# Column means of an 8192 x 8192 matrix: loads in pairs of row groups on two queues, without early loads, the last four groups summed by TensorE alone

## The chip, the cores and the metric

The kernel runs on one core of one Trainium2 chip. The metric is the device time of one execution in microseconds (us). "SyncE", "ScalarE", "GpSimd", "VectorE" and "TensorE" are the engines that the profile writes as SP, ACT, POOL, DVE and PE. "DMA" is the core's 16 DMA engines, which move data between device memory and the on-chip buffers; a transfer is put to them by an instruction on SyncE's or ScalarE's instruction stream.

## The reference

```python
def setup_inputs():
    return {"x": np.random.randn(8192, 8192).astype(np.float32)}

def reference(x):
    return np.mean(x, axis=0)
```

The input is 268.4 MB of float32, every byte of which has to be read once; the output is 32 KB.

## The kernel before

The 8192 rows are 64 groups of 128 rows (`G = 64`, `P = 128`). A group is 4 MB: 128 partitions with a row of 8192 columns each. The buffer `bufs` has six slots of one group each: slots 0 to 3 take loads, slot 4 is `both`, slot 5 is the running sum `acc`. Columns are counted in blocks of `F = 512`; `W = 128`.

**The stream.** A load of two groups (8 MB) lets partition p take two neighbouring rows, so it reads 64 KB in one piece per partition. Two pairs of slots, 0-1 and 2-3, are filled in turn. For each pair VectorE does two adds of 8192 columns: `both = slot + slot`, after which the pair of slots is free, and `acc = acc + both`. Line 96 has all adds of VectorE, line 76 all loads. All loads are issued by SyncE, so they stand in one queue (q1 in the profile). The load into a pair of slots is issued when the `both` add that reads it has ended; the load of the other pair is then still in flight.

**Waits.** An add that needs both a load and the add before it waits for a no-op on another engine (line 99), which waits for the two; the no-ops are on ScalarE and on GpSimd. `declare_no_dep` takes away dependences that such a wait covers already. A load with an even number from 8 on also waits for the loads eight and seven before it (`over`), which have long landed by then.

**The beginning.** The first load brings four groups, the second two more into the slots of `both` and `acc`. Around them SyncE issues two early loads into a tile `early`: columns 14F to 16F of group 60 and 9F to 14F of group 63. GpSimd adds them to `acc` in two pieces in the middle of the stream (line 129).

**The end.** From group 56 on the loads bring one group each. VectorE adds groups 56 to 59, 14 blocks of group 60 and blocks 7 to 15 of group 61. GpSimd adds three blocks of group 62 (line 148). TensorE sums `acc` and what is left of groups 61, 62 and 63 over the partitions (line 183): the matrix `ones`, holding 1/8192, times a block gives sums, in PSUM tiles `bank` (two), `wide`, `two` and `last`. ScalarE copies them out (line 198), VectorE the last one (line 214). Stores are issued by SyncE and ScalarE (line 201; those of ScalarE are q10). Group 63 is loaded in four pieces of 1 MB, 1 MB, 512 KB and 256 KB, so that little work follows the last piece. `keep_in_program_order` keeps the order on an engine as written.

Of the kernel before, what the change touches and what calls it, by code (L numbers as in the profile page):

```python
# [9 lines left out]
def kernel(  # L10
# [2 lines left out]
    x: bass.AP,  # L13
    out: bass.AP,
):

    nc = tc.nc
    f32 = mybir.dt.float32
    M, N = x.shape  # L40
    P = nc.NUM_PARTITIONS
    F = 512
    W = F // 4
    G = M // P
    U = 6
    sync = mybir.DependencyInfo(mybir.DependencyClass.Sync, mybir.DependencyReason.DATA)

    sb = ctx.enter_context(tc.tile_pool(name="sb", bufs=1))
    psp = ctx.enter_context(tc.tile_pool(name="psum", bufs=1, space=bass.MemoryType.PSUM))

    bufs = sb.tile([P, U, N], f32, name="bufs")
    both = bufs[:, U - 2, :]
    acc = bufs[:, U - 1, :]
    ones = sb.tile([P, 32], f32, name="ones")
    early = sb.tile([P, 7 * F], f32, name="early")
    tail = sb.tile([P, W], f32, name="tail")
    warm = sb.tile([P, 32], f32, name="warm")
    nc.gpsimd.memset(ones[:], 1.0 / M)  # L58
    ready = sb.tile([P, 1], f32, name="ready")
    tc.keep_in_program_order(  # L60
        nc.gpsimd.tensor_add(out=ready[:], in0=ones[:, 0:1], in1=ones[:, 1:2]))  # L61
    banks = [psp.tile([P, F], f32, name=f"bank{b}") for b in range(2)]
    wide = psp.tile([P, 2 * F], f32, name="wide")
    two = psp.tile([P, 2 * W], f32, name="two")
    last = psp.tile([P, W], f32, name="last")

    loads = []

    def landed(*inss):

        nop = tc.keep_in_program_order(nc.sync.nop()).ins
        for o in inss:
            tc.add_manual_dep(nop, o.name, sync, reason="SyncE waits")

    def load(dst, src):
        ins = tc.keep_in_program_order(nc.sync.dma_start(out=dst, in_=src)).ins  # L76
        k = len(loads)
        over = loads[k - 8:k - 6] if k >= 8 and k % 2 == 0 else []
        tc.declare_no_dep(ins, group="loads", keep=over, reason="the reader of the buffer waited")
        for o in over:  # L80
            tc.add_manual_dep(ins, o.name, sync, reason="covers the next load too")
        tc.add_to_no_dep_group("loads", ins)
        loads.append(ins)
        return ins

    def rows(g, n=1):
        return x[g * P:(g + n) * P, :]

    def load_rows(g, u, n):
        return load(bufs[:, u:u + n, :], rows(g, n).rearrange("(p j) c -> p j c", j=n))  # L90

    adds, joins = [], {}

    def add(dst, a, b, dmas):

        ins = nc.vector.tensor_add(out=dst, in0=a, in1=b).ins  # L96
        if dmas and adds:
            waiter = nc.scalar if len(adds) % 8 > 1 else nc.gpsimd
            nop = joins[waiter] = tc.keep_in_program_order(waiter.nop()).ins  # L99
            for o in dmas + adds[-1:]:  # L100
                tc.add_manual_dep(nop, o.name, sync, reason="the no-op waits")
            for group in ("loads", "adds"):
                tc.declare_no_dep(ins, group=group, reason="the no-op waited")
            tc.add_manual_dep(ins, nop.name, sync, reason="waits for both at once")
        elif adds:
            tc.declare_no_dep(ins, group="loads", reason="the add ahead waited")
        tc.declare_no_dep(ins, group="early", reason="the no-op waited, or the add behind it")
        tc.add_to_no_dep_group("adds", ins)
        adds.append(ins)

    load(early[:, 5 * F:], rows(G - 4)[:, 14 * F:])
    first, second = load_rows(0, 0, 4), load_rows(4, 4, 2)
    load(early[:, :5 * F], rows(G - 1)[:, 9 * F:14 * F])
    add(bufs[:, 2:4, :], bufs[:, 2:4, :], bufs[:, 0:2, :], [first])
    add(bufs[:, 4:6, :], bufs[:, 4:6, :], bufs[:, 2:4, :], [second])
    add(acc, acc, both, [])
    tc.keep_in_program_order(nc.scalar.copy(out=warm[:], in_=ones[:]))  # L117
    ahead = []
    g = 6
    while g < G - 8:  # L120
        u = (g + 2) % 4
        dma = load_rows(g, u, 2)
        add(both, bufs[:, u, :], bufs[:, u + 1, :], [dma])
        add(acc, acc, both, ahead)
        ahead = []
        if g in (24, 32):
            lo, hi = (0, 4) if g == 24 else (4, 7)
            cols = slice((9 + lo) * F, (9 + hi) * F)
            ins = tc.keep_in_program_order(nc.gpsimd.tensor_add(  # L129
                out=acc[:, cols], in0=acc[:, cols], in1=early[:, lo * F:hi * F])).ins  # L130
            tc.add_to_no_dep_group("early", ins)
            ahead = [ins]
        g += 2

    while g < G - 4:
        row = bufs[:, (g + 2) % 4, :]
        add(acc, acc, row, [load(row, rows(g))])
        g += 1
    for lo, hi, loaded in [(0, 14, 14), (7, 16, 16)]:
        row = bufs[:, (g + 2) % 4, :]  # L140
        dma = load(row[:, :loaded * F], rows(g)[:, :loaded * F])
        cols = slice(lo * F, hi * F)
        add(acc[:, cols], acc[:, cols], row[:, cols], [dma])
        g += 1
    r61, r62, r63 = [bufs[:, (g + 1 + j) % 4, :] for j in range(3)]
    load(r62, rows(g))
    for cols in [slice(14 * F, 16 * F), slice(8 * F, 9 * F)]:
        joined = tc.keep_in_program_order(nc.gpsimd.tensor_add(  # L148
            out=acc[:, cols], in0=acc[:, cols], in1=r62[:, cols])).ins
    g += 1  # L150
    for lo, hi in [(4, 8), (0, 4), (14, 16), (8, 9)]:
        load(r63[:, lo * F:hi * F], rows(g)[:, lo * F:hi * F])

    sums = []

    def blocks(row, lo, hi):
        for i in range(lo, hi):
            sums.append((banks[i // 4], i % 4, 0, row[:, i * F:(i + 1) * F]))

    def spread(dst, row, lo, hi, part=slice(None)):  # L160
        n = (hi - lo) * W
        for c in range(0, n, F)[part]:
            for q in range(4):
                at = lo * F + q * n + c
                sums.append((dst, q, c, row[:, at:at + min(F, n - c)]))

    blocks(acc, 2, 5)
    blocks(acc, 0, 2)
    blocks(r61, 0, 7)
    blocks(acc, 5, 8)  # L170
    blocks(r62, 0, 8)
    spread(wide, acc, 9, 14, slice(1))
    blocks(r63, 4, 8)
    spread(wide, r62, 9, 14, slice(1))
    for row in (acc, r62):
        spread(wide, row, 9, 14, slice(1, 2))
    spread(two, acc, 14, 16)
    blocks(r63, 0, 4)
    spread(last, acc, 8, 9)
    spread(two, r63, 14, 16)  # L180
    spread(last, r63, 8, 9)
    for n, (dst, q, c, cols) in enumerate(sums):
        summed = tc.keep_in_program_order(nc.tensor.matmul(  # L183
            out=dst[32 * q:32 * q + 32, c:c + cols.shape[1]],
# [5 lines left out]
            skip_group_check=True,  # L190
        )).ins

    res = both[:, :2 * F].rearrange("p (b c) -> p b c", b=2)
    res5 = both[:, 2 * F:2 * F + 5 * W]
    res2 = both[:, 4 * F:4 * F + 2 * W]

    def copy(dst, src):
        return tc.keep_in_program_order(nc.scalar.copy(out=dst, in_=src)).ins  # L198

    def store(engine, dst, src, *then):  # L200
        ins = tc.keep_in_program_order(engine.dma_start(out=dst, in_=src)).ins
        for o in then:
            tc.add_manual_dep(ins, o.name, sync, reason="follows that load")
        return ins

    def part(lo, hi):
        return out[lo * F:hi * F].rearrange("(q c) -> q c", q=4)

    copy(res[:, 1, :], banks[1][:])
    s1 = store(nc.scalar, part(4, 8), res[0:P:32, 1, :], loads[-4])  # L210
    copy(res5, wide[:, :5 * W])
    copy(res[:, 0, :], banks[0][:])
    copied = copy(res2, two[:])
    ended = nc.vector.tensor_copy(out=tail[:], in_=last[:]).ins  # L214
    landed(*joins.values())
    s5 = store(nc.sync, part(9, 14), res5[0:P:32, :], *loads[-7:-3])
    s0 = store(nc.sync, part(0, 4), res[0:P:32, 0, :])
    s2 = store(nc.scalar, part(14, 16), res2[0:P:32, :])
    store(nc.sync, part(8, 9), tail[0:P:32, :])
    landed(loads[-2], joined)  # L220
    landed(loads[-1], copied)
    landed(s0, s5)
    landed(s1, summed)
    landed(s2, ended)
    hold = tc.keep_in_program_order(nc.vector.nop()).ins
    tc.add_manual_dep(hold, s0.name, sync, reason="VectorE ends late")

# [29 lines left out]
```

## Time and profile before

| | |
|---|---|
| time, median of 3 runs | 628.55 us (627.99 to 628.99) |
| profiled execution, span from first to last instruction | 626.4 us |
| what lies around the span (runs less span) | 1.6 to 2.6 us, 2.15 at the median |
| read from device memory | 268.44 MB, 429 GB/s over the span |
| VectorE busy | 529.3 us (85%) |
| TensorE busy | 13.3 us (2%) |
| ScalarE, GpSimd busy | 3.7 us, 12.0 us |
| granted TensorE clock | 1.000 |

The time of the profiled execution is not listed apart from the three runs; its span is the part that the profile explains. The DMA share is the mean busy share of the 16 DMA engines, and can pass 1 in a short window, because a packet counts where it starts. A wait is shown with the instruction that released it. A value such as "DVE bufs<-bufs L96" names the engine, the output and input tiles and the line. The profile records a float32 matmul of this kernel twice, so its 126 records are 63 matmuls of the program.

### The profile page before, as it was taken

The numbers are of one execution on the slowest core, as the hardware profiler recorded it, in microseconds if no ns is written. First come the engines' busy times: TensorE is split into PE (matmuls) and PEld (weight loads), VectorE is DVE, ScalarE is ACT, GpSimd is POOL, SyncE is SP. The second block draws the span as 40 slices with busy tenths as digits, with TensorE's granted clock in tenths as the row PEclk, the third lists the DMA queues.
The fourth block names the chain that finished last, engine by engine and source line by source line (L and its number), as shares of the span: only waits on it lengthen the run. The fifth ranks groups of instructions, "written<-read, shape, count | busy, mean of one in ns | idle before, by whom it ended". The sixth has DMA issues, their size and how long they took to land.

```text
span 626.4 us, 484 instructions
## 1 busy us (share of the span) xinstructions
PE 13.3 (2%) x126; PEld 4.0 (1%) x126; DVE 529.3 (85%) x60; ACT 3.7 (1%) x6; POOL 12.0 (2%) x10
## 2 busy tenths in 40 slices
PE   0000000000000000000000000000000000000008
PEld 0000000000000000000000000000000000000002
DVE  0028999998888998889998899888898888999992
ACT  0000000000000000000000000000000000000001
POOL 0000000000000000020000200000000000000002
PEclk9999999999999999999999999999999999999999
DMA  8999999999999999999999999999999999999997
GB/s 372 465 402 428 459 410 460 402 469 402 469 402 469 402 469 402 469 402 469 402 465 406 439 431 427 444 410 460 402 469 402 469 402 469 402 435 435 419 435 305
DMA packets 5930, 268.50 MB, mean 429 GB/s; under 512 B 660, under 2 KB 668, under 8 KB 1064
## 3 DMA queue, kind: packets, MB, share of 16 engines
q1 hardware_dynamic: 5912, 268.46, 99.3%
q8 instruction: 1, 0.02, 0.0%
q10 hardware_dynamic: 16, 0.01, 0.0%
q14 instruction: 1, 0.01, 0.0%
HBM read 268.44 MB, written 0.03 MB: 429 GB/s over the span
## 4 chain that ended last, share of the span: by engine, by line
DMA 59%; DVE 30%; another core or an unknown queue 10%; issue 0%; SPq 0%; ACTq 0%; PE 0%; POOL 0%; POOLq 0%
DMA bufs<-in_x_dram 59%; DVE bufs L96 30%; SPq L76 0%; ACTq L99 0%; PE last L183 0%; DVE tail L214 0%; POOL ready L61 0%; POOL ones L58 0%; POOLq L99 0%; POOLq L241 0%
## 5 line engine op out<-in xcount | busy, mean ns | idle before, releaser
L96 DVE TENSOR_TENSOR bufs<-bufs 128x8192 f32<-128x8192 f32 (+3 forms) x59 | 529.0, 8966 | 85.9 <-DMA bufs<-in_x_dram 43.0
L183 PE MATMUL bank<-bufs,ones 128*32 128x512 f32 x62 | 10.0, 716 | 610.3 <-DVE bufs L96 610.0
L129 POOL TENSOR_TENSOR bufs<-bufs,early 128x2048 f32<-128x2048 f32 (+1 forms) x2 | 7.9, 3954 | 348.5 <-DVE bufs L96 348.5
L148 POOL TENSOR_TENSOR bufs<-bufs 128x1024 f32<-128x1024 f32 (+1 forms) x2 | 3.6, 1824 | 258.9 <-DMA bufs<-in_x_dram 258.9
L214 DVE COPY tail<-last 128x128 f32<-128x128 f32 x1 | 0.3, 291 | 8.8 <-PE last L183 8.8
L183 PEld LDWEIGHTS bank<-bufs,ones 128*32 128x32 f32 x62 | 2.2, 121 | 616.4 <-issue 614.5
L198 ACT COPY bufs<-bank 128x512 f32<-128x512 f32 x2 | 1.2, 586 | 617.9 <-PE bank L183 617.9
L183 PE MATMUL wide<-bufs,ones 128*32 128x512 f32 (+1 forms) x32 | 2.5, 432 | 0.0
L117 ACT ACT_TABLE_LOAD x1 | 1.3, 1283 | 0.7 <-PEq L241 0.7
L183 PE MATMUL two<-bufs,ones 128*32 128x256 f32 x16 | 1.2, 380 | 0.0
L183 PEld LDWEIGHTS wide<-bufs,ones 128*32 128x32 f32 x32 | 1.0, 110 | 1.8 <-issue 1.8
L183 PE MATMUL last<-bufs,ones 128*32 128x128 f32 x16 | 0.8, 279 | 0.1
L198 ACT COPY bufs<-wide 128x640 f32<-128x640 f32 x1 | 0.7, 692 | 1.1 <-PE wide L183 1.1
L183 PEld LDWEIGHTS last<-bufs,ones 128*32 128x32 f32 x16 | 0.4, 109 | 1.2 <-issue 0.6
L183 PEld LDWEIGHTS two<-bufs,ones 128*32 128x32 f32 x16 | 0.4, 109 | 0.1
L198 ACT COPY bufs<-two 128x256 f32<-128x256 f32 x1 | 0.4, 372 | 0.1
L117 ACT COPY warm<-ones 128x32 f32<-128x32 f32 x1 | 0.2, 217 | 0.0
L61 POOL TENSOR_TENSOR ready<-ones 128x1 f32<-128x1 f32 x1 | 0.2, 193 | 0.1
L58 POOL MEMSET ones<- 128x32 f32 x1 | 0.1, 125 | 0.3 <-POOLq L241 0.3
L241 POOL MEMSET const-float32-0.0<- 128x1 f32 x1 | 0.1, 98 | 0.2 <-issue 0.2
L241 POOL MEMSET const-bfloat16-1.0<- 128x1 bf16 x1 | 0.1, 102 | 0.0
L241 POOL MEMSET const-uint8-127<- 128x1 uint8 x1 | 0.1, 102 | 0.0
(1 smaller groups left out, 0.1 us busy)
## 6 DMA issues: line engine op xcount, KB each, us to landing
bufs<-in_x_dram SPq DMA_DIRECT2D x6, 4096.0 KB, 20.4
bufs<-in_x_dram SPq DMA_DIRECT2D x1, 3584.0 KB
bufs<-in_x_dram SPq DMA_DIRECT2D x2, 1024.0 KB, 18.7
early<-in_x_dram SPq DMA_DIRECT2D x1, 1280.0 KB
early<-in_x_dram SPq DMA_DIRECT2D x1, 512.0 KB
bufs<-in_x_dram SPq DMA_DIRECT2D x1, 512.0 KB, 19.4
bufs<-in_x_dram SPq DMA_DIRECT2D x27, 29.9
bufs<-in_x_dram SPq DMA_DIRECT2D x1, 256.0 KB, 19.7
```

What stands on the lines that cost most here:

```text
L58: nc.gpsimd.memset(ones[:], 1.0 / M)
L61: nc.gpsimd.tensor_add(out=ready[:], in0=ones[:, 0:1], in1=ones[:, 1:2]))
L96: ins = nc.vector.tensor_add(out=dst, in0=a, in1=b).ins
L117: tc.keep_in_program_order(nc.scalar.copy(out=warm[:], in_=ones[:]))
L129: ins = tc.keep_in_program_order(nc.gpsimd.tensor_add(out=acc[:, cols], in0=acc[:, cols], in1=early[:, lo * F:hi * F])).ins
L148: joined = tc.keep_in_program_order(nc.gpsimd.tensor_add(out=acc[:, cols], in0=acc[:, cols], in1=r62[:, cols])).ins
L183: summed = tc.keep_in_program_order(nc.tensor.matmul(out=dst[32 * q:32 * q + 32, c:c + cols.shape[1]], lhsT=ones[:], rhs=cols, start=all(( ...
L198: return tc.keep_in_program_order(nc.scalar.copy(out=dst, in_=src)).ins
L214: ended = nc.vector.tensor_copy(out=tail[:], in_=last[:]).ins
L241: nc = _bacc.Bacc("TRN2", target_bir_lowering=False, num_devices=1)
```

## The change

Loads 0 to 30 bring two groups each; load 31 brings group 62, loads 32 to 35 the pieces of group 63 (2 MB, 1.25 MB, 512 KB, 256 KB). Loads 3, 5, ... 29 are issued by ScalarE, all others by SyncE, so in the stream slots 0-1 are filled from SyncE's queue and slots 2-3 from ScalarE's. Each load still waits for the `both` add that read its slots. The early loads, the first load of four groups, the single-group loads and all adds of GpSimd are gone. All no-ops ahead of adds are on GpSimd. VectorE adds groups 0 to 59 with 59 adds of 8192 columns; TensorE sums groups 60, 61, `acc`, 62 and 63 in that order, 24 matmuls each, 120 in all. VectorE also copies one of the two 512-column results. The results have tiles of their own, and the stores have no added waits on loads.

```diff
     def load(dst, src):
-        ins = tc.keep_in_program_order(nc.sync.dma_start(out=dst, in_=src)).ins
         k = len(loads)
+        engine = nc.scalar if 2 <= k < G // 2 - 1 and k % 2 else nc.sync
+        ins = tc.keep_in_program_order(engine.dma_start(out=dst, in_=src)).ins
         over = loads[k - 8:k - 6] if k >= 8 and k % 2 == 0 else []
...
-            waiter = nc.scalar if len(adds) % 8 > 1 else nc.gpsimd
+            waiter = nc.gpsimd
...
-    load(early[:, 5 * F:], rows(G - 4)[:, 14 * F:])
-    first, second = load_rows(0, 0, 4), load_rows(4, 4, 2)
-    load(early[:, :5 * F], rows(G - 1)[:, 9 * F:14 * F])
...
+    def pair(g):
+        u = g % 4
+        dma = load(bufs[:, u:u + 2, :], rows(g, 2).rearrange("(p j) c -> p j c", j=2))
+        return bufs[:, u, :], bufs[:, u + 1, :], dma
+
+    a, b, dma = pair(0)
+    add(acc, a, b, [dma])
     tc.keep_in_program_order(nc.scalar.copy(out=warm[:], in_=ones[:]))
...
+    for g in range(2, G - 4, 2):
+        a, b, dma = pair(g)
+        add(both, a, b, [dma])
+        add(acc, acc, both, [])
+    r60, r61, _ = pair(G - 4)
+    r62, r63 = bufs[:, 2, :], bufs[:, 3, :]
+    load(r62, rows(G - 2))
+    for lo, hi in [(0, 8), (8, 13), (13, 15), (15, 16)]:
+        load(r63[:, lo * F:hi * F], rows(G - 1)[:, lo * F:hi * F])
...
+    for row in (r60, r61, acc, r62, r63):
+        blocks(banks[0], row, 0)
+        blocks(banks[1], row, 4)
+        spread(banks[2], row, 8, 5)
+        spread(banks[3], row, 13, 2)
+        spread(last, row, 15, 1)
...
+    copy(0)
+    nc.vector.tensor_copy(out=res[1][:], in_=banks[1][:])
+    copy(2)
+    copied = copy(3)
     ended = nc.vector.tensor_copy(out=tail[:], in_=last[:]).ins
     landed(*joins.values())
+    s0 = store(nc.sync, 0, 4, res[0])
+    s4 = store(nc.sync, 4, 8, res[1])
+    s8 = store(nc.sync, 8, 13, res[2])
+    s13 = store(nc.scalar, 13, 15, res[3])
+    store(nc.sync, 15, 16, tail)
```

More of the change, by code (lines that the diff above doesn't have):

```diff
@@ L54 @@
     ones = sb.tile([P, 32], f32, name="ones")
-    early = sb.tile([P, 7 * F], f32, name="early")
     tail = sb.tile([P, W], f32, name="tail")
+    res = [sb.tile([P, w], f32, name=f"res{i}") for i, w in enumerate((F, F, 5 * W, 2 * W))]
     warm = sb.tile([P, 32], f32, name="warm")
@@ L61 @@
         nc.gpsimd.tensor_add(out=ready[:], in0=ones[:, 0:1], in1=ones[:, 1:2]))
-    banks = [psp.tile([P, F], f32, name=f"bank{b}") for b in range(2)]
-    wide = psp.tile([P, 2 * F], f32, name="wide")
-    two = psp.tile([P, 2 * W], f32, name="two")
+    banks = [psp.tile([P, w], f32, name=f"bank{b}") for b, w in enumerate((F, F, 2 * F, 2 * W))]
     last = psp.tile([P, W], f32, name="last")
@@ L87, in rows @@
         return x[g * P:(g + n) * P, :]
-    def load_rows(g, u, n):
-        return load(bufs[:, u:u + n, :], rows(g, n).rearrange("(p j) c -> p j c", j=n))
     adds, joins = [], {}
@@ L106, in add @@
             tc.declare_no_dep(ins, group="loads", reason="the add ahead waited")
-        tc.declare_no_dep(ins, group="early", reason="the no-op waited, or the add behind it")
         tc.add_to_no_dep_group("adds", ins)
         adds.append(ins)
-    load(early[:, 5 * F:], rows(G - 4)[:, 14 * F:])
-    first, second = load_rows(0, 0, 4), load_rows(4, 4, 2)
-    load(early[:, :5 * F], rows(G - 1)[:, 9 * F:14 * F])
-    add(bufs[:, 2:4, :], bufs[:, 2:4, :], bufs[:, 0:2, :], [first])
-    add(bufs[:, 4:6, :], bufs[:, 4:6, :], bufs[:, 2:4, :], [second])
@@ L116 @@
-    add(acc, acc, both, [])
-    tc.keep_in_program_order(nc.scalar.copy(out=warm[:], in_=ones[:]))
[L118 to L149, printed above, removed]
@@ L150 @@
-    g += 1
-    for lo, hi in [(4, 8), (0, 4), (14, 16), (8, 9)]:
-        load(r63[:, lo * F:hi * F], rows(g)[:, lo * F:hi * F])
-    sums = []
[L156 to L162, printed above, removed]
-            for q in range(4):
-                at = lo * F + q * n + c
-                sums.append((dst, q, c, row[:, at:at + min(F, n - c)]))
@@ L167 @@
[L167 to L181, printed above, removed]
+    def pair(g):
+        u = g % 4
+        dma = load(bufs[:, u:u + 2, :], rows(g, 2).rearrange("(p j) c -> p j c", j=2))
+        return bufs[:, u, :], bufs[:, u + 1, :], dma
@@ new lines, with blocks @@
+    a, b, dma = pair(0)
+    add(acc, a, b, [dma])
+    tc.keep_in_program_order(nc.scalar.copy(out=warm[:], in_=ones[:]))
+    for g in range(2, G - 4, 2):
[7 more added lines that the diff above has]
+        load(r63[:, lo * F:hi * F], rows(G - 1)[:, lo * F:hi * F])
+    sums = []
+    def blocks(dst, row, lo):
+        for q in range(4):
+            sums.append((dst, q, 0, row[:, (lo + q) * F:(lo + q + 1) * F]))
@@ L182, with spread @@
+    def spread(dst, row, lo, n):
+        for c in range(0, n * W, F):
+            for q in range(4):
+                at = lo * F + q * n * W + c
+                sums.append((dst, q, c, row[:, at:at + min(F, n * W - c)]))
+    for row in (r60, r61, acc, r62, r63):
[4 more added lines that the diff above has]
+        spread(last, row, 15, 1)
     for n, (dst, q, c, cols) in enumerate(sums):
@@ L191, with copy, store @@
         )).ins
[L193 to L213, printed above, removed]
+    def copy(i):
+        return tc.keep_in_program_order(nc.scalar.copy(out=res[i][:], in_=banks[i][:, :res[i].shape[1]])).ins
+    def store(engine, lo, hi, src):
+        dst = out[lo * F:hi * F].rearrange("(q c) -> q c", q=4)
+        return tc.keep_in_program_order(engine.dma_start(out=dst, in_=src[0:P:32, :])).ins
+    copy(0)
+    nc.vector.tensor_copy(out=res[1][:], in_=banks[1][:])
+    copy(2)
+    copied = copy(3)
     ended = nc.vector.tensor_copy(out=tail[:], in_=last[:]).ins
     landed(*joins.values())
[L216 to L220, printed above, removed]
+    s0 = store(nc.sync, 0, 4, res[0])
[3 more added lines that the diff above has]
+    store(nc.sync, 15, 16, tail)
+    landed(loads[-2])
     landed(loads[-1], copied)
-    landed(s0, s5)
-    landed(s1, summed)
-    landed(s2, ended)
+    landed(s0, s4)
+    landed(s8, summed)
+    landed(s13, ended)
     hold = tc.keep_in_program_order(nc.vector.nop()).ins
```

## The prediction

> **What bounds the kernel now.** I read the page first, for which resource never rests:
>
> ```profile
> PE 13.3 (2%) x126; PEld 4.0 (1%) x126; DVE 529.3 (85%) x60; ACT 3.7 (1%) x6; POOL 12.0 (2%) x10
> ...
> DMA  8999999999999999999999999999999999999997
> ...
> q1 hardware_dynamic: 5912, 268.46, 99.3%
> ...
> q10 hardware_dynamic: 16, 0.01, 0.0%
> ```
>
> The DMA row is full from the second slice to the next to last, and SyncE's queue q1 holds the 16 engines for 99.3% of the span. VectorE has 15% to spare. Next, the windows, one cycle of two loads (16.78 MB) each:
>
> ```profile
> 123.78:162.48 38.70, 0.00 (x0) 0.00 (x0) 34.76 (x4) 0.00 (x0) 0.00 (x0) 1.00 1.00 434
> 162.48:201.18 38.70, 0.00 (x0) 0.00 (x0) 34.77 (x4) 0.00 (x0) 0.00 (x0) 1.00 1.00 434
> 394.70:433.40 38.70, 0.00 (x0) 0.00 (x0) 34.77 (x5) 0.00 (x0) 0.00 (x0) 1.00 1.00 434
> ```
>
> The columns after the window are its length, busy times of the engines, granted clock, DMA share, GB/s. Every cycle is 38.70 us, 19.35 a load, with the DMA share at 1.00; four adds take 34.8. The chain of waits shows why the queue never empties:
>
> ```profile
> 123.78 8.70 DVE bufs L96
> 132.48 0.02 issue
> 132.50 29.93 DMA bufs<-in_x_dram
> 162.42 0.03 ACTq L99
> 162.46 0.02 issue
> 162.48 8.70 DVE bufs L96
> ```
>
> An add frees two slots, the next load is issued at 132.50 and lands 29.93 us later: 10.6 behind the load still in flight, 19.35 of its own. So an add can be 10 us late and nothing is lost. Last, the timeline of the end:
>
> ```profile
> 623.23 0.43 PE L183 MATMUL last<-bufs,ones 128*32 128x128 f32 x8
> 623.63 0.51 ACTq L201 DMA_DIRECT2D out_dram<-bufs  x1
> 623.73 0.29 DVE L214 COPY tail<-last 128x128 f32<-128x128 f32 x1 [8.83 <-PE last L183]
> 624.04 0.50 SPq L201 DMA_DIRECT2D out_dram<-tail  x1
> ```
>
> The last piece is seen landed at 623.19; matmuls, copy and store of 2 KB take 3.2 us to 626.4. So the span is 1.8 us to the first packet, 620.9 of packets without a gap (the trace's packet records run from 1.78 to 622.65), 0.54 until the landing is seen, and a tail of 3.2. The change pays only through these four.
>
> **Part 1, the packets.** Each engine serves 8 partitions of every load. The packet records have medians of 2.421 us for 64 KB, 1.218 for 32 KB, 1.067 for 28 KB, 0.385 for 10 KB, 0.313 for 8 KB, 0.159 for 4 KB, 0.084 for 2 KB, and 0.007 for a load's closing semaphore write. Before, an engine has 224 + 48 + 8 + 8 + 16 + 16 + 8 of these and 40 closing writes: 542.3 + 58.5 + 8.5 + 3.1 + 5.0 + 2.5 + 0.7 + 0.3 = 620.9, which is what the records span. After, 31 loads of two groups give 248 packets of 64 KB, group 62 gives 8 of 32 KB, group 63 8 each of 16, 10, 4 and 2 KB, with 36 closing writes. With 16 KB at 0.615 (an estimate, between the rows of 10 and 28 KB): 600.4 + 9.7 + 4.9 + 3.1 + 1.3 + 0.7 + 0.25 = 620.3. Fewer, larger packets save **0.55 us**. Without early loads the same bytes come later, so nothing else is won.
>
> **Part 2, two queues.** Bytes do not change, but from load 3 on two rings can be active on each engine, and the load issued later no longer stands behind the earlier one. What matters is whether an engine ever runs dry. After a load completes, 0.45 us pass until its add starts (closing writes end at 123.33, the add starts at 123.78), the add takes 8.70 and 0.02 to the issue, and the first packet comes 1.04 after the issue (0.74 to 1.78 at the start): 10.2 us. Take equal sharing. If the other load needs r more us alone when a load completes, it has r - 10.2 left as the new one joins, takes twice that, and the new one then has 29.55 - r left. At the beginning loads 0, 1 and 2 are in one queue. Load 3 joins when load 2 has 9.15 left; load 2 completes 18.3 later with 10.2 of load 3 left; load 4 joins 10.2 later, exactly as load 3 ends. No gap, but no margin either. From there VectorE is a little behind (two adds of load 2, 17.4 us, before load 3's): load 5 joins 17.4 after load 4, load 6 finds 3.8 left of load 5, and then r alternates between 15.55 and 14.0, completions 20.9 and 17.8 apart. Each interval is longer than VectorE's 17.4, and the margin against running dry is 3.8 us or more. ScalarE's issue is dearer than SyncE's 0.33 (0.51 and 1.07 in the rows of its two stores), up to 0.7 us, which the 3.8 cover; at the tie of loads 3 and 4 a later ScalarE load leaves more to cover, not less. A late issue of load 4 there would cost its own length once; SyncE's issues range from 0.33 to 0.47, so 0 to 0.14. I take 0.
>
> The page has no two loads on two rings at once. Shared time is 9.15 us a load on average, 3.8 packets, and from load 3 to 29 about **100 packets per engine**. From below: if one ring's packet hides the fixed part of the other's (2 x 1.218 - 2.421 = 0.015 us a packet), 100 x 0.015 = 1.5 us are won. From above: beside ScalarE's stores near 622.4 the 2 KB packets of loads take 0.084 to 0.092, 0.008 more: 0.8 us; the farthest row is the longest 64 KB packet of the stream, 2.560 against 2.421: 100 x 0.139 = 14 us. The row of real neighbours is the nearest, and its 0.008 is within the scatter of 2 KB packets; I take 0.
>
> The Trainium skill's page "DMA: Bandwidth & Descriptors", section "Issuing engines are not separate DMA queues", says that DMAs from different engines run on the same 16 DMA engines and interleave, saving only issue time; here issues already lie under the stream, so by it this part yields nothing either way. Its section "Queues, rings and completion order" has each engine take turns between rings packet by packet, which speaks for the equal sharing; the records near 622.4 (q10's packets between q1's) agree, but with 2 KB packets only.
>
> **Part 3, ScalarE and GpSimd.** ScalarE's queue holds only the loads until the final copies, so a load that waits there blocks nobody; the copies need TensorE 14 us and more after load 29 is issued. No-ops on GpSimd hand over in 0.04 us like ScalarE's (0.03). GpSimd's adds go; they stretched two VectorE adds (11.21 and 10.12 in the chain against 8.70), under cover. No path term: 0. Were the cover gone, they would have been worth 3.9.
>
> **Part 4, VectorE.** 59 adds at 8.70, 513 us, and one copy of 0.6. Per load 17.4 against 19.35 of DMA: covered. After load 29 completes, near 588, `acc` is final near 606, 17 us before the last landing.
>
> **Part 5, TensorE and the end.** 120 matmuls against 63. At the start of its work before, TensorE put out four 512-column matmuls per 0.86 us, later per 0.43. A row of groups is three such sets of 512, one of 256, two of 128: 3.4 us cold, 1.7 warm. Groups 60 and 61 land near 602.5 and take at most 6.8; `acc` is done by 613; group 62 lands at 612 and is done by 616, before 2 MB of group 63 land at 617.7. The sets on the 1.25 MB and 512 KB pieces take 1.3 and 0.4 at the cold rate, against 1.9 and 0.7 between landings. ScalarE's copy of 640 columns (0.69) then ends some 0.1 after the last landing; SyncE's store of it, 0.64, is issued by 0.75, ahead of the tail store at 0.85. So the tail stays 3.2 us, up to 0.3 longer if that store is late, or 0.2 if the last matmuls run cold. The value is 0.
>
> **Sum.** 626.4 - 0.55 + 0 = 625.85 for the span; with the 2.15 around it (1.6 to 2.6 over the runs) **628.0 us**. About 0.2%, or 1.26 us, is what a measurement of this kernel can tell from no change, so the forecast is "same", 627.3 to 629.8.
>
> **Rivals.** (a) *Turns between rings cost.* A packet that follows one of another ring pays an extra price, from a break in the engine's run of reads. It decides from (1.26 + 0.55) / 100 = 0.018 us a packet; 0.05 gives 633.0, the farthest row 642. For it: no row shows two loads mixing, and single 64 KB packets do take 0.1 longer in the first 60 us. Against it: neighbours of 2 KB show at most 0.008. (b) *Rings overlap.* The 0.015 per packet is hidden: 626.5. For it: packets of one ring follow each other with this fixed part throughout; against: bytes alone take 2.406 of 2.421. (c) *Sharing is not equal.* If the newcomer went first, load 2 would end behind load 3; VectorE, which takes loads in order, would free nothing meanwhile, and DMA would idle 10.2 us in each cycle of two loads: 14 x 10.2 = 143 us more, 771. It decides when the margin of 3.8 us is used up. Against it: q10's stores beside the last loads did not push them aside. (d) *The tail:* its late store plus cold matmuls, +0.5, inside the forecast.
>
> **How the numbers follow.** Same, with parts 2 to 5 at nothing: 0.49. Rival (a) above its point: 0.30; (c): 0.03; these are slower, 0.33 together. Rival (b), nearly whole: 0.18, faster. The likeliest case's own range is 627.3 to 629.8. The range reaches down to 626.6, as (b) with the runs' scatter asks, and up to 632.5, an extra 0.045 us a packet, leaving out about half of (a) and all of (c). 628.0 is the likeliest case.
>
> **What would show it.** Right: q1 and q10 with nearly half the bytes each (14 of 31 pair loads, 117 MB, on q10); the DMA row full in all middle slices; cycles of two loads of 38.7 us, with completions unevenly spaced; first add near 22 us; last landing near 622.7. Wrong by (a): cycles over 38.7 at a DMA share still 1.00, fewer GB/s. By (b): cycles under 38.6. By (c): slices of the DMA row well below 9 and long waits of VectorE on GpSimd's no-op. By the tail: more than 3.5 us from the last landing to the end.

## The result, and the profile after

| | before | after |
|---|---|---|
| time, median | 628.50 us (627.99 to 628.99, 13 runs) | 629.55 us (629.21 to 630.37, 13 runs) |
| ratio | | 1.0018, 95% interval 1.0011 to 1.0025 |
| span of the profiled execution | 626.4 us | 628.0 us |
| last landing, as TensorE sees it | 623.23 | 624.71 |

The change costs 1.05 us, 0.18%. (The profiled execution after took 629.90, 0.35 above the median.) The result is inside the band called "same" and inside the range, but the forecast was a gain of half a microsecond, and the loss is clear of the noise. The page after:

```profile
PE 20.1 (3%) x240; PEld 7.8 (1%) x240; DVE 513.8 (82%) x61; ACT 3.1 (0%) x5; POOL 0.5 (0%) x6
...
DMA  9999999999999999999999999999999999999996
...
q1 hardware_dynamic: 3200, 151.03, 55.8%
q10 hardware_dynamic: 2024, 117.45, 43.2%
q8 instruction: 2, 0.03, 0.0%
q14 instruction: 1, 0.01, 0.0%
```

The bytes are split over q1 and q10 as forecast, and the DMA row is full. The cycles of two loads, in windows (length, busy times, clock, DMA share, GB/s):

```profile
163.41:202.10 38.69, 0.00 (x0) 0.00 (x0) 34.76 (x4) 0.00 (x0) 0.00 (x0) 1.00 1.00 434
395.61:434.31 38.70, 0.00 (x0) 0.00 (x0) 34.77 (x4) 0.00 (x0) 0.00 (x0) 1.00 1.00 434
```

They are what they were, 38.70. So the middle is not where the time went. The end of the chain of waits after:

```profile
599.29 23.52 DMA bufs<-in_x_dram
622.81 0.04 issue
622.86 1.86 PE bank L119 x24
624.72 0.46 PE last L119 x8
625.18 0.02 issue
625.20 0.29 DVE tail L140
```

The last piece of 256 KB is seen at 624.71 instead of 623.23. From there to the end it is 3.3 us, against 3.2: nearly the whole 1.6 us between the two spans lies ahead of the last landing. The packet records say where. Of the 16 DMA engines, those that nothing disturbed begin the closing semaphore write of the last load by 622.64; before it was 622.67. One engine comes at 624.22. It fell behind here, in the DMA view cut to 614 to 616 us:

```profile
q1 hardware_dynamic: 54, 0.88, 105.3%
q8 instruction: 1, 0.02, 3.3%
```

One 16 KB packet of kind "instruction" on q8, starting at 614.64 and taking 1.06 us, went over one of the engines that carry the loads, and the 16 KB load packet behind it took 1.11 us where its neighbours take 0.61. I call such a packet a fetch: by its kind it brings instructions, and the experiments ask for which engine. Of the closing writes of the load under way (the 2 MB piece of group 63), fourteen come at 617.12 to 617.63, one at 618.28 and one at 619.24. The one at 618.28 had been 0.6 behind since an 8 KB packet on q14 at 464.84. Before, the only q8 packet inside the span comes at 622.56, when that engine has no load left to bring, and the first q14 packet at 626.03.

### The profile page after: what moved, and what is told of

Read it like the earlier page. It is cut to its first block, busy times and chain, and to the rows that moved or that the text cites. A ratio compares the mean times of both kernels' runs of the same rounds, so it can differ in the third digit from the quotient of the medians.

```text
span 628.0 us, 700 instructions
## 1 busy us (share of the span) xinstructions
PE 20.1 (3%) x240; PEld 7.8 (1%) x240; DVE 513.8 (82%) x61; ACT 3.1 (0%) x5; POOL 0.5 (0%) x6
## 4 chain that ended last, share of the span: by engine, by line
DMA 75%; DVE 24%; PE 0%; issue 0%; SPq 0%; POOLq 0%
DMA bufs<-in_x_dram 75%; DVE bufs L68 24%; PE bank L119 0%; SPq L53 0%; POOLq L71 0%; PE last L119 0%; DVE tail L140 0%
## 5 line engine op out<-in xcount | busy, mean ns | idle before, releaser
L68 DVE TENSOR_TENSOR bufs<-bufs 128x8192 f32<-128x8192 f32 x59 | 512.8, 8692 | 94.3 <-POOLq L71 69.3
L119 PE MATMUL bank<-bufs,ones 128*32 128x512 f32 (+2 forms) x200 | 19.6, 535 | 605.0 <-DMA bufs<-in_x_dram 605.0
L119 PEld LDWEIGHTS bank<-bufs,ones 128*32 128x32 f32 x200 | 6.7, 118 | 615.9 <-issue 614.1
L130 ACT COPY res<-bank 128x512 f32<-128x512 f32 (+2 forms) x3 | 1.6, 552 | 621.4 <-PE bank L119 621.4
L119 PE MATMUL last<-bufs,ones 128*32 128x128 f32 x40 | 2.1, 275 | 0.0
```

The lines of the kernel that those rows point to most:

```text
L119: summed = tc.keep_in_program_order(nc.tensor.matmul(out=dst[32 * q:32 * q + 32, c:c + cols.shape[1]], lhsT=ones[:], rhs=cols, start=all(( ...
L130: return tc.keep_in_program_order(nc.scalar.copy(out=res[i][:], in_=banks[i][:, :res[i].shape[1]])).ins
```

## The experiments

**1. The same with one queue.**

```diff
-        engine = nc.scalar if 2 <= k < G // 2 - 1 and k % 2 else nc.sync
+        engine = nc.sync
```

> The changed kernel with all loads issued by SyncE again, nothing else altered. Theory A (an instruction fetch of TensorE, 16 KB on q8, falls into the stream at 614.64 us instead of behind it at 622.56, and puts one DMA engine 1.5 us behind the others): the matmuls and their place are the same, so the fetch stays at 614 to 615 us and the time stays at 629.2 to 629.7. Theory B (turns between two rings cost time): with one ring the price is gone, 628.0 to 628.4. If the gap of about 0.3 us where load 4 joins as load 3 ends (80.1 us) is a real loss, A gives 629.2 rather than 629.5.

Measured: 629.35 us against 628.21 (1.0018, 1.0010 to 1.0027), the same loss as with two queues. The q8 packet is at 615.05. Turns between rings are not the cause. The chain of waits of this run shows something else:

```profile
603.97 5.87 PE bank L119 x40
609.84 0.22 PE last L119 x8
610.06 3.22 PE bank L119 x40
...
620.39 3.52 PE bank L119 x40
623.91 0.45 PE last L119 x8
```

TensorE has work nearly without a pause from 604 to 624.4, 3.4 us for each group even when warm. The prediction had 1.7. So TensorE is nearly as late as the late engine's data. Here it ends the chain itself, by little: its last weight load still waits 0.46 us for the last piece, which is seen at 623.89.

**2. Fewer matmuls by more adds.** VectorE adds groups 60 and 61 too; TensorE keeps 60 matmuls.

```diff
-    for g in range(2, G - 4, 2):
+    for g in range(2, G - 2, 2):
...
-    r60, r61, _ = pair(G - 4)
...
+    columns(r62, range(4))
+    columns(r63, [0])
+    columns(acc, range(4))
+    columns(r63, range(1, 4))
```

> The changed kernel, two queues kept; VectorE adds groups 60 and 61 as well, so that TensorE has only group 62, the first 8 blocks of group 63, the running sum and the rest of group 63: 60 matmuls instead of 120. Theory A: the fetch comes after about 215 records of TensorE's work, which are now reached only with the last two pieces, near 622.7 us, behind the stream; the last landing falls from 624.67 to about 623.2 us, and the time by 1.2 to 1.5 us to 628.0 to 628.4 (0.3 more if the later sum of the accumulator lengthens the tail). Theory B: two rings still take turns, 629.3 to 629.8.

Measured: 636.91 us against 628.21 (1.0129, 1.0114 to 1.0145). The design was at fault: VectorE still had the adds of groups 58 and 59 to do when groups 60 and 61 landed, so the accumulator was final only at 624.6, and most of TensorE's work came behind that. As a test of the time it says nothing. The packets do say something: q8's came at 626.23, behind the loads, and the last load was in at 623.26 instead of 624.22. One engine alone is late there, by 0.6, as q14's packet at 464.80 had left one.

**3. The fetch alone, added to the kernel before.**

```diff
+    spare = psp.tile([P, 32], f32, name="spare")
+    for n in range(24):
+        tc.keep_in_program_order(nc.tensor.matmul(
+            out=spare[0:32, :], lhsT=ones[:], rhs=ones[:], start=True, stop=True,
+            tile_position=(0, 0), skip_group_check=True))
```

> The kernel before with 24 small matmuls added at its very beginning, on 32 columns of the constant tile into a spare PSUM tile that nobody reads. They end within the first few us and only move TensorE's place in its instruction stream by 96 records. Theory A: the 16 KB fetch moves from 622.56 to 616 to 618 us, into the stream, and the time rises by 1.0 to 1.6 us to 629.5 to 630.1. Theory B: one ring, nothing to pay, 628.3 to 628.7.

Measured: 629.32 us against 628.21 (1.0017, 1.0008 to 1.0026), +1.11 at the medians, as much as the whole change. The runs scatter widely, from 628.27 to 630.69, so the size is known only to the width of the interval; why they scatter is not shown. Its timeline, and its DMA view from 619 to 621 us:

```profile
0.91 2.77 PE L184 MATMUL spare<-ones 128*32 128x32 f32 x48 [0.91 <-POOL ones L58]
...
624.20 0.16 PEld L188 LDWEIGHTS last<-bufs,ones 128*32 128x32 f32 x8 [0.48 <-DMA bufs<-in_x_dram]
```

```profile
q1 hardware_dynamic: 140, 0.78, 95.6%
q8 instruction: 1, 0.02, 3.4%
```

The added matmuls are over at 3.7 us. Six hundred microseconds later q8's packet comes at 619.65 instead of 622.56, and the last landing is seen at 624.20 instead of 623.23. The packet belongs to TensorE's place in its program, not to the time: when it starts, 114 matmul records have begun in the kernel before, 108 in the changed kernel and 110 here, 48 of them the added ones. It is not an exact count of matmuls begun: over the other runs the first q8 packet comes when 98 to 128 records have begun, but 68 in run 2 and 88 and 92 in runs 13 and 14.

**4. Two such fetches in the stream.** The changed kernel with 40 of these matmuls at its beginning.

> The changed kernel with 40 such small matmuls at the beginning, 160 records. Theory A: the first fetch moves to about 608 us and the second from 623.93 to 616 to 618 us, so both fall into the stream. If both come over the same DMA engine the delays add: 1.0 to 1.5 us more than the changed kernel, 630.6 to 631.0; if over two engines only the slower counts, 629.5. Theory B: unchanged, 629.3 to 629.8.

Measured: 629.73 us (1.0028, 1.0017 to 1.0040), little above the changed kernel. The q8 packets are at 607.52 and 619.95. In the last load two engines are late, both until about 623.8: the fetches went over two engines, so the delays stand side by side and do not add. TensorE, again nearly without a pause, ends the chain, though its last weight load waits 0.47 us for the last piece, seen at 624.27.

**5 to 8. With less for TensorE to do.** Groups 60 and 61 are loaded and left out of the sum; a group takes 20 matmuls.

```diff
-    for row in (r60, r61, acc, r62, r63):
+    for row in (acc, r62, r63):
...
-        spread(banks[2], row, 8, 5)
-        spread(banks[3], row, 13, 2)
+        blocks(banks[2], row, 8)
+        spread(banks[3], row, 12, 3)
```

> The changed kernel (two queues) in which TensorE sums only the accumulator, group 62 and group 63; groups 60 and 61 are loaded but left out of the sum. The column layout is cut so that a group takes 20 matmuls, 60 in all. The fetch of 16 KB comes after some 52 matmuls, so now with the second piece of group 63, near 621.5 us or later. Theory A (the fetch delays the last landing): the last landing is seen near 623.2 instead of 624.67 and the time is 628.2 to 628.6. Theory C (beside or instead of the fetch, TensorE itself is late, since 120 matmuls from 604 us need 20 us): this run removes both, so the same. Theory B (turns between rings cost): still 629.3 or more.

> The run before with 24 small matmuls at its beginning into a spare tile, so that the fetch falls back to about 615 us while TensorE has as little to do at the end; groups 60 and 61 left out of the sum again. Theory A: 1.0 to 1.5 us more than without them, near 629.5. Theory C alone (TensorE late, the fetch harmless): no difference.

> The kernel with groups 60 and 61 left out of the sum and 60 matmuls, but all loads from SyncE's queue. What two queues cost without either lateness: if the meeting of loads 3 and 4 (a gap at 80 us) costs 0.3 us, this is 0.3 faster than the two-queue form, 627.9 to 628.2; if turns between rings cost nothing at all, equal.

> The one-queue form (groups 60 and 61 left out of the sum) with the no-ops ahead of the adds shared between ScalarE and GpSimd as in the kernel before. All runs of the changed form show an 8 KB fetch on q14 at 462 to 465 us that puts one DMA engine 0.6 us behind; the kernel before shows none there. If the 29 no-ops on GpSimd bring it on, it leaves the stream here, the last landing comes up to 0.6 us earlier and the time falls to 627.4 to 627.8; if it has another cause, it stays and the time is that of the one-queue form.

Measured: 629.64 (1.0026, 1.0015 to 1.0038), 630.19 (1.0029, 1.0018 to 1.0041), 629.70 (1.0022, 1.0013 to 1.0030) and 629.78 us (1.0022, 1.0013 to 1.0031), all against 628.29. The first missed its 628.2 to 628.6. Its last landing did come down, to 623.6 (one engine is still 0.4 late, as in run 2), but ScalarE's final store took 1.37 us to issue (0.51 before) and its packets were now the last. The timelines of runs 5 and 6:

```profile
623.58 0.18 PEld L119 LDWEIGHTS last<-bufs,ones 128*32 128x32 f32 x8 [0.47 <-DMA bufs<-in_x_dram]
...
624.38 1.37 ACTq L134 DMA_DIRECT2D out_dram<-res  x1
```

```profile
624.34 0.17 PEld L124 LDWEIGHTS last<-bufs,ones 128*32 128x32 f32 x8 [0.48 <-DMA bufs<-in_x_dram]
```

Moving the fetch back into the stream (run 6, q8 at 617.30) puts the last landing from 623.58 to 624.34, +0.76, and the median by 0.55. One queue instead of two (run 7): no difference that shows (629.70 against 629.64). Run 8 clears GpSimd's no-ops: the q14 packet stays, at 462.0.

**9 and 10. Whose is the q14 packet?** Eight one-column memsets on VectorE ahead of the changed kernel's first load, and 24 ahead of the kernel before.

> The changed kernel with 8 one-column memsets of a spare tile on VectorE at the very beginning, when it has nothing to do for 22 us. The question is whose instruction stream brings on the 8 KB fetch on q14 near 464.8 us, which puts one DMA engine 0.6 us behind. Theory D (it is VectorE's): 8 instructions are four loads' worth of adds, so the fetch moves about 77 us earlier, to 385 to 390. Rival (SyncE's, or none of the two): it stays at 464 to 465.

> The kernel before with 24 such memsets on VectorE at the beginning. Before, the first fetch on q14 comes at 626.03, behind everything. Theory D: it now falls into the stream and costs about 0.6 us, 628.8 to 629.0. Rival: no fetch on q14 before 626, 628.3.

Measured: in the changed kernel it moves from 464.84 to 387.09, by 77.8 us, four loads of 19.35 as foretold (629.49 us, one run). In the kernel before it appears at 253.44, here in the DMA view from 253 to 255 us, and costs 0.83 us at the medians: 629.05 against 628.22 (1.0010, 1.0001 to 1.0019).

```profile
q1 hardware_dynamic: 16, 1.05, 123.1%
q14 instruction: 1, 0.01, 1.0%
```

Run 10's last landing, in its timeline, is 0.46 later than the 623.23 before:

```profile
623.69 0.16 PEld L186 LDWEIGHTS last<-bufs,ones 128*32 128x32 f32 x8 [0.47 <-DMA bufs<-in_x_dram]
```

So the packet is VectorE's. In every run that has it in the stream, 47 of VectorE's records come before it.

**11. One VectorE instruction less.**

```diff
-    nc.vector.tensor_copy(out=res[1][:], in_=banks[1][:])
+    copy(1)
```

> The changed kernel with the second 512-column result copied by ScalarE instead of VectorE: one instruction less in VectorE's stream, as many as in the kernel before. Theory E (the kernel before has no q14 fetch inside the stream because its VectorE program is just short enough to need no further block, and the added copy is what makes it need one): the fetch near 464.8 us is gone. Rival: it stays. The 16 KB fetch of TensorE at 614 to 615 is still there and goes over another DMA engine, so the last landing stays near 624.5 and the time near 629.2 to 629.6 either way.

Measured: the packet at 464.8 is gone; the first on q14 is at 626.20. The second copy on VectorE was what brought it on. But the time rose, to 630.58 us against 628.34 (1.0040, 1.0027 to 1.0054). Now the q14 packet lies beside the last stores: the closing write of ScalarE's is over at 626.71, and SyncE's step that waits for it begins at 627.58, 0.88 later; before, SyncE's step behind the last closing write began 0.03 later.

**12. Neither fetch.** Run 5 with the second copy and an early store on ScalarE (groups 60 and 61 left out).

> Two queues, groups 60 and 61 left out of the sum as before (60 matmuls, so that TensorE's fetch comes behind nearly all of the stream), the second result copied by ScalarE, and ScalarE's dear first store (1.07 to 1.37 us of issue) put early, so that its last one is the second, as in the kernel before. If the two fetches and the late store are the whole loss: no fetch inside the stream before 621 us, the last landing near 623.2, and a time of 628.0 to 628.5, level with the kernel before. If two queues or the missing early loads cost something of their own: 629 or more.

Measured: 630.37 us against 628.34 (1.0036, 1.0023 to 1.0049), a miss. q8's packet came at 621.96, on an engine that still had the last 2 KB packets to bring: they start 0.21 us apart instead of 0.08, and the landing is seen at 624.5. q14's came at 626.18 beside the last store, whose closing write was over at 626.78 and was followed by SyncE at 627.65, 0.87 later, as in run 11.

**13 and 14. Both fetches behind everything.** From run 12: the accumulator's first 8 blocks left out as well, and VectorE's end tied to the last store; then the same with one queue.

```diff
+        if row is not acc:
+            blocks(banks[0], row, 0)
+            blocks(banks[1], row, 4)
...
-    tc.add_manual_dep(hold, s0.name, sync, reason="VectorE ends late")
+    tc.add_manual_dep(hold, s15.name, sync, reason="VectorE ends late")
```

> Two queues; groups 60 and 61 and the accumulator's first 8 blocks are left out of TensorE's sum, so it has 52 matmuls and its fetch comes with the last ones; VectorE's end waits for the last store, so its fetch comes behind that. If the fetches were the whole loss, the last landing is near 622.7 in the packets (623.2 as seen), the tail 3.2 us, the time 627.7 to 628.3. If two queues cost something of their own, 628.8 or more.

> The same with one queue. If turns between rings cost nothing but the meeting of loads 3 and 4 costs its 0.3 us, 0 to 0.3 us less than with two queues; if two queues overlap and win, more.

Measured: 629.01 (1.0012, 1.0003 to 1.0021) and 629.11 us (1.0014, 1.0005 to 1.0023) against 628.21. The DMA view of run 13 from 3 to 622.3 us has no instruction packet (q8's starts at 622.32, on an engine that has no load left to bring), and the timeline shows the landing back where it was:

```profile
q1 hardware_dynamic: 3110, 149.89, 56.0%
q10 hardware_dynamic: 2016, 117.44, 43.8%
```

```profile
623.23 0.18 PEld L120 LDWEIGHTS last<-bufs,ones 128*32 128x32 f32 x8 [0.47 <-DMA bufs<-in_x_dram]
...
624.24 0.50 SPq L135 DMA_DIRECT2D out_dram<-tail  x1
```

623.23, to the hundredth the value before, with two queues and without early loads. The 0.8 that is left lies behind it: SyncE issues the last store at 624.24 instead of 624.04, being busy with another, and VectorE, tied to the last store by this run's own edit, drains at 626.53, 0.4 after SyncE. That these make up the whole 0.8 is read from the timeline, not tested. Two queues and one are level for the third time.

## Why the prediction was wrong

**The step that failed: what stands on the DMA engines.** The sum in part 1 counted loads and closing writes only. The page before showed q8 and q14 with one packet each at 0.0% of the span, and I passed them over:

```profile
q8 instruction: 1, 0.02, 0.0%
...
q14 instruction: 1, 0.01, 0.0%
```

What matters is not their share but their place: no engine rests, so a packet of 1.06 us put into one engine's row makes every load that follows 1 us or more later, as a load has landed when its slowest engine is done. The change moved both. TensorE's 120 matmuls reach the point of the fetch at 614 instead of 622.5 (part 5 priced their time, not their instructions), and VectorE's added copy (part 4: "one copy of 0.6", covered) brought on a fetch in the stream (run 11). Run 3 shows the first at +1.11, run 10 the second at +0.83, each alone on the kernel before. In the changed kernel they go over two engines, so it pays the larger: one engine 1.6 us behind, the other 0.6. With the larger one gone, the last load was in 0.96 us sooner (run 2).

The Trainium skill has the mechanism: "Runtime: NRT & Kernel Launch", section "Instruction fetch mechanics", says that an engine's instructions are refilled in blocks of 16 KiB over DMA, and that crossing a boundary is mostly hidden. The sizes agree for q8 (16 KB; q14's are 8 KB); "hidden" does not hold here, where nothing is hidden that takes an engine of the stream (+1.11 us in run 3).

**Part 1, the saving of 0.55:** did not arrive. Summed from the records, an engine's load packets take 621.6 us after and 621.8 before, 0.1 less. The sixteen first packets, now of 64 KB, take 3.03 us each instead of 2.42, 0.61 that the sum did not have (it also has a closing write at 0.007; the records have 0.009). The 64 KB packets between 45 and 100 us average 2.4325 instead of 2.4197; that is not the second queue, as runs 1 and 14 with one queue have 2.4196 and 2.4463. That the sum of medians met the span of 620.9 before was luck: the records add up to 0.9 more, and each packet begins some 0.003 us before the one ahead has ended. Run 13 has nearly the same packets (group 63 is cut a little differently) and lands exactly with the kernel before.

**Part 2, two queues at nothing:** right as far as the runs can tell: three pairs (after and 1, 5 and 7, 13 and 14) differ by -0.20, +0.06 and +0.10 us at the medians, with intervals of half a microsecond or more either way. Rivals (a), (b) and (c) fall with them: cycles stay at 38.7, and 100 packets in turn with another ring cost and win nothing that shows. The equal sharing came close: in the stream loads complete 21.7 and 16.9 us apart in turn, where 20.9 and 17.8 were forecast. At the tie of loads 3 and 4 no engine ran dry: load 3's closing writes are at 80.07 to 80.41, and on each engine load 4's first packet starts within 0.01 us of the closing write, from 80.07.

**Part 3, GpSimd's no-ops at nothing:** right (run 8).

**Part 5, TensorE:** mis-sized by a factor of two. The timeline before has rows such as these:

```profile
616.73 0.13 PEld L183 LDWEIGHTS bank<-bufs,ones 128*32 128x32 f32 x4 [0.30 <-issue]
617.16 0.13 PEld L183 LDWEIGHTS bank<-bufs,ones 128*32 128x32 f32 x4 [0.30 <-issue]
```

I read four records per 0.43 us as four matmuls, but a matmul has two records, as the front says; so four take 0.86 warm and a group 3.4, not 1.7. TensorE ends group 62 at 620.3, not 616. This too would have cost something: by an estimate from 620.26, when it begins group 63, and the 3.22 that the 20 matmuls ahead of a group's last four take without waits (run 1's chain), it could begin on the last piece at 623.5, 0.25 later than before, even if no piece were late. In the profile after the pieces are later than that (624.71), so the fetch decides there; in runs 1 and 4 the two are within 0.3. The tail of 3.2 held: 3.3. The loads' times in parts 4 and 5 were put about 1.2 us early (load 29 ends at 589.2, groups 60 and 61 are in at 603.7), which touched nothing in the sum.

What is open: a form of the changed kernel that sums all groups, has both fetches out of the way and pays nothing in the tail was not built, so that it would be level with the kernel before is shown for its landing (run 13), not for its time. No run pointed to a version faster than the kernel before.

## What to carry to other kernels

When a kernel keeps all DMA engines busy from end to end, list everything else that goes over them, down to packets of 0.0% share: here an instruction fetch cost its time or more where it fell into the stream, and nothing in the landing where it fell behind it. A change that adds or moves instructions, even one copy on an engine with time to spare, can move those fetches; look at where the instruction packets start before and after. And count what one record of the profile is before multiplying by it.

## What the runs showed of the hardware

- TensorE's 16 KB fetch comes with its place in the program: in the changed kernel when 108 and again when 224 of its 240 matmul records have begun (614.64 and 623.93). Beside loads the first one takes 1.04 to 1.11 us, and the load packet behind it on the engine loses another half (1.11 for 0.61). Two in one run went over two DMA engines (run 4).
- VectorE's 8 KB fetch (0.32 us by its record) puts its engine 0.6 us behind the others for the rest of the stream; the 64 KB load packet that follows it on the engine takes 3.08 instead of 2.42.
- Whether VectorE fetches at all inside the kernel hung on one instruction: with 61 on the page it fetches in the stream, with 60 it does not (after and run 11).
- With a fetch beside the last stores, SyncE went on 0.87 to 0.88 us after the closing write that it waited for (runs 11 and 12), against 0.03 to 0.10 before and after (0.35 in run 5, without a fetch there).
- ScalarE's first small store costs 1.07 to 1.37 us of issue, a second one 0.51 to 0.52, even where the queue has issued 14 loads before.
